# The second branch's output projection as seven half-size products instead of eight, in a hybrid decoder layer

## The chip, the cores and the metric

One core of a Trainium2 chip runs the whole layer. The time is device microseconds of one execution. An execution under the hardware profiler gives the views that are quoted here; their times are microseconds unless marked ns. The engines are PE (TensorE matmuls; PEld its weight loads), DVE (VectorE), ACT (ScalarE), POOL (GpSimd) and SP (SyncE), which here only issues transfers.

## The reference

```
h = rmsnorm(x, norm_g)
proj = h @ w_in                       # q, k, v, gates of both branches, merge logits
...
y_a = o_gla @ w_pa                    # first branch: gated linear attention
...
o_sb = stick_breaking(...)            # second branch, 8 heads of 128
o_sb = o_sb.reshape(B, T, SB_WIDTH) * jax.nn.silu(s_gate)
y_b = o_sb @ w_pb
gates = jax.nn.sigmoid(m_logits + b_gate).reshape(B, T, N_BRANCH, D_MODEL)
merged = gates[:, :, 0] * y_a + gates[:, :, 1] * y_b
x = x + merged @ w_o
return rmsnorm(x, final_g)
```

SEQ and D_MODEL are 1024, everything is float32. The change concerns `o_sb @ w_pb` and, through the buffers, `merged @ w_o`.

## The kernel before

Every float32 operand of a matmul is split into a high part (rounded to the matmul's format by ScalarE) and a low part (what is left, subtracted by VectorE), and a product takes three matmuls: high by high, high by low, low by high. Each matmul has 128 rows of contraction and 512 columns. Activations are kept transposed, with the width on the partitions, in quarters: `A11`, `A12`, `A21`, `A22` are first or second half of the tokens by even or odd blocks of 128 of the width, each a tile of 4 x 512 in high and low.

The stages follow one another on TensorE. The norm and the first values come first. Then 28 jobs of two projections each (`pair_job`, `Pairs`) run as seven half-size products with sums and differences of quarters (Strassen's scheme in Winograd's form): a job is seven units of twelve matmuls, with the sums of the weights made by GpSimd. During the first 49 units VectorE also computes the decays of the linear attention and, from unit 22 on, the sums of `w_o` that the last stage uses: `t_load` fetches two blocks of rows, `t_sum` makes four differences, `t_store` writes them to DRAM (`d_t`). The list `tjobs` says after which unit each of these is issued, in a part where the order on ScalarE and VectorE is that of the program. Then the linear attention (GLA) runs with four units between its steps, and what is left of the 196 units follows. The paired products of the linear attention's q and k multiply by a factor `f` that is loaded from `d_e` (L554).

Stick-breaking attention (L895 to L1089) goes through 64 steps, eight heads of eight blocks. A step issues the scores two steps ahead, then transposes its weights (`turn`); `values(h, 0)` multiplies the weights of the first half of the queries with v after step 4, `values(h, 1)` after step 0 of the next head. Units of two other projections, 24 matmuls each, lie between (`Line`): the gates of this branch, then `pa`, the output projection of the first branch; 26 are placed in and before this stage, and six `pa` units are left behind it, in the order of output blocks 5, 6, 7, both halves of the tokens of each.

The projection of the second branch, `pb_unit`, has 16 units: eight output blocks by two halves of the tokens, each with eight blocks of contraction and three matmuls. The gated heads come back from DRAM (`d_osb`), are split into four quarters `bq`, and each output block's weights are loaded and split two blocks ahead. `m_half` evicts a unit: it loads the second gate and the first branch's gated part (`d_gb`, `d_ma`), takes the sigmoid on ScalarE, and VectorE multiplies (L1141) and adds (L1142). After every fourth unit GpSimd makes the four sums S1, S2, S4, S3 of the merged blocks (L1152), which go to DRAM and come back for the last stage.

The output projection is seven half-size products already: items `(u, t)`, product u for block t of 128 tokens, twelve matmuls each, in an order written out by hand (`items`, `parts`, `loads`, L1343 to L1354). `parts[k]` names which high and low parts are made around item k (`o_hi` on ScalarE, L1203; `o_lo` on VectorE, L1207), `loads[k]` what is fetched. In this stage the order on ScalarE, VectorE and TensorE is that of the program; SP's order, and everything before this stage's loop, is set by the scheduler of the framework. VectorE adds a bank to the residual y (L1275); the last items scale and store the rows.

Of the kernel before, what the change touches and what calls it, by code (L numbers as in the profile page):

```python
# [15 lines left out]
P = 128  # L16
# [25 lines left out]
WARM = (13, 4)  # L42

# [56 lines left out]
def hybrid_layer(ctx: ExitStack, tc: tile.TileContext, x, norm_g, w_in, w_up, b_dec,  # L100
# [34 lines left out]
    d_t = dram_set("t", 4, [P, 4, HALF])  # L135
    d_s = {nm: dram_set("s" + nm, 2, [P, 2, HALF]) for nm in ("S1", "S2", "S3", "S4", "A22")}
# [564 lines left out]

    wt = {}
    tq_ctx = ExitStack()
    tq = tq_ctx.enter_context(tc.tile_pool(name="tq", bufs=3, reuse_waits="tile"))

    def t_load(j):
        wt[j] = tq.tile([P, 4, HALF], F32, tag="t", name="t")
        for two in range(2):
            nc.sync.dma_start(wt[j][:, 2 * two:2 * two + 2],
                              w_o[(2 * j + two) * P:(2 * j + two + 1) * P].rearrange("p (h c) -> p h c", h=2))  # L710

    def t_sum(j, i):
        dst, x1, x2_ = ((0, 1, 0), (1, 3, 1), (3, 3, 0), (2, 2, 3))[i]
        nc.vector.tensor_sub(wt[j][:, dst], wt[j][:, x1], wt[j][:, x2_])

    def t_store(j):
        nc.sync.dma_start(d_t[j][:], wt[j])

    tjobs = [[] for _ in range(49 - len(djobs))]
    for j in range(4):  # L720
        tjobs[5 * j].append((t_load, (j,)))
# [345 lines left out]
    for eb in range(KB):  # L1067
        line += ([pa(eb, 0)] if eb > 2 else []) + [pa(eb, 1)] + ([pa_load(eb + 3)] if eb + 3 < KB else [])
# [7 lines left out]
    for s, (h, i) in enumerate(steps):  # L1076
        if i % 2 == 0 and s + 4 < len(steps):
            h2, i2 = steps[s + 4]
            load_q(h2, i2 // 2)
        if i == 1 and h + 1 < SB_H:  # L1080
            load_head(h + 1)
        if s + 2 < len(steps):
            scores(*steps[s + 2])
        st.run(SB_PLAN[i][0])
        turn(h, i)
        st.run(SB_PLAN[i][1])
        if i % 4 == 0 and s:
            values(*((h, 0) if i else (h - 1, 1)))
# [5 lines left out]

    pq = ctx.enter_context(tc.tile_pool(name="pq", bufs=1, reuse_waits="tile"))
    fg = pq.tile([P, D], F32, tag="fg", name="fg", bufs=1)
    nc.sync.dma_start(fg, final_g.partition_broadcast(P))
    ssq = pq.tile([P, NT, 2], F32, tag="ssq", name="ssq", bufs=1)
    mo_ctx = ExitStack()
    mo = mo_ctx.enter_context(tc.tile_pool(name="mo", bufs=6, reuse_waits="tile"))  # L1100
    pb_ctx = ExitStack()
    pb = pb_ctx.enter_context(tc.tile_pool(name="pb", bufs=1, side="right", reuse_waits="tile"))
    bq = {k: quarter(pb, "b", f"b{k[0]}{k[1]}") for k in hq}

    def b_dma(j):
        reload_dma((d_osb[2 * j], d_osb[2 * j + 1]), j)

    def pb_load(eb):
        return load(w_pb, eb * P, ("b", eb))

    def pb_unit(eb, n):
        return unit(("b", eb), bq, n, lambda pt: m_half(pt, eb, n))

    b_dma(0)
    b_dma(1)
    st.run(1)
    reload_split(bq, 0, 0)
    b_dma(2)
    st.run(1)
    reload_split(bq, 1, 1)  # L1120
    b_dma(3)
    st.run(1)
    reload_split(bq, 2, 2)
    pb_load(0)[0]()
    st.run(1)
    reload_split(bq, 3, 3)
    pb_load(1)[0]()
    st.run()


    op = {"A11": quarter(hp, "mA11", "a11"), "A12": quarter(hp, "mA12", "a12"),
          "B11": quarter(hp, "wB11", "a22"), "B21": quarter(a21b, "wB21", "a21")}
    ms, oraw = {}, {}

    def m_half(pt, eb, n):
        j, e = divmod(eb, 2)
        o = stage().bitcast(F32)
        merge_gate(o[:, 0], d_gb, 8, eb, n)
        nc.sync.dma_start(o[:, 1], d_ma[eb][:, half(n)])
        m = ms[j, n, e] = mo.tile([P, HALF], F32, tag="m", name="m")  # L1140
        nc.vector.tensor_mul(o[:, 0], pt, o[:, 0])  # L1141
        nc.vector.tensor_add(m, o[:, 0], o[:, 1])  # L1142
        if n == 0:
            hi, lo = op[("A11", "A12")[e]]
            split(m, hi[:, j], lo[:, j])

    def m_sum(j, nm, x1, x2_, fn):

        def go():
            a, b_ = (ms[j, v] if isinstance(v, str) else ms[(j,) + v] for v in (x1, x2_))  # L1150
            ms[j, nm] = ev.tile([P, HALF], F32, tag="f", name="f")
            nc.gpsimd.tensor_tensor(ms[j, nm], a, b_, op=fn)  # L1152

        return (go, False)

    def m_sums(j):
        return [m_sum(j, "S1", (1, 0), (1, 1), ALU.add), m_sum(j, "S2", "S1", (0, 0), ALU.subtract),
                m_sum(j, "S4", (0, 1), "S2", ALU.subtract), m_sum(j, "S3", (0, 0), (1, 0), ALU.subtract)]

    def m_stores(j, nms=("S2", "S1", "S4", "S3", "A22")):  # L1160
        def go():
            for nm in nms:
                nc.sync.dma_start(d_s[nm][j // 2][:, j % 2], ms[j, nm] if nm[0] == "S" else ms[j, 1, 1])

        return (go, False)


    WQ = {"B11": (0, 0), "B21": (1, 0), "B22": (1, 1)}

    def o_load(nm, tag="raw", js=(0, 4)):  # L1170
        def go():
            raw = (raw_tile().rearrange("p k c -> p (k c)") if tag == "raw" else
                   sw.tile([P, 4, 4, P], F32, tag="tt", name="tt", bufs=1).rearrange("p q a c -> p (q a c)"))
            oraw[nm] = raw = raw.rearrange("p (j c) -> p j c", j=4)
            if nm[0] == "T":
                for j in range(4):
                    nc.sync.dma_start(raw[:, j], d_t[j][:, ("T1", "T3", "T4", "T2").index(nm)])
                return
            for i in range(2):
                n = min(js[1] - 2 * i, 2)  # L1180
                if nm in WQ:
                    e, J = WQ[nm]
                    src = (w_o.rearrange("(j two p) c -> two p j c", two=2, p=P)
                           [e][:, 2 * i:2 * i + 2, J * HALF:(J + 1) * HALF])
                else:
                    src = d_s[nm][i][:]
                nc.sync.dma_start(raw[:, 2 * i:2 * i + n], src[:, 0:n])

        return (go, False)

    def o_ends(nm, js):

        j0, n = (js, 1) if isinstance(js, int) else (js[0], 2)
        src = ms[j0, nm] if (nm, j0) in (("S2", 3), ("S1", 3)) else oraw[nm][:, j0:j0 + n]
        if n == 1:
            src = src if (nm, j0) in (("S2", 3), ("S1", 3)) else src[:, 0]
        hi, lo = (op[nm][j0 // 2] if isinstance(op[nm], list) else
                  tuple(a[:, j0:j0 + n] if n > 1 else a[:, j0] for a in op[nm]))
        return hi, lo, src
# [9 lines left out]
    def o_part(nm, i):  # L1209
        def go():  # L1210
            o_hi(nm, (2 * i, 2 * i + 1))
            o_lo(nm, (2 * i, 2 * i + 1))
# [195 lines left out]
```

## Time and profile before

| | |
|---|---|
| three runs | 1212.0, 1212.16, 1214.72 us; median 1212.16 |
| profiled execution, whole | 1212.76 us |
| its span, first to last instruction | 1211.1 us, granted clock 0.998 |
| last matmul of the first branch's six units, about | 1040 us |
| second branch's projection | about 1040 to 1127 us |
| output projection | about 1127 to 1204 us |

In lists by line, a row has line, engine, operation, output and inputs, shapes and count, then busy time in us and mean ns, then the engine's idle time before these instructions and what ended it. In lists by time, a row has start, duration, engine, line, and in brackets the idle time before. A row of waits has the waiting engine and tile, the releaser, the total in us, how often, and the longest. In the table by stage, the count of instructions stands in brackets behind each engine's busy time.

### The profile page before, as it was taken

What the parts mean: (1) busy time and instruction counts of PE and PEld (TensorE: products, weight loads), DVE (VectorE), ACT (ScalarE), POOL (GpSimd) and SP (SyncE); (2) the same over time, 40 slices, a digit from 0 to 9 for tenths busy, and PEclk for the clock granted to TensorE, in tenths of its full rate; (3) what the DMA queues carried; (4) which work ended last, traced back from release to release, by engine and by line L of the source; (5) the groups of instructions that cost most, each with busy time, mean ns of one, the idle gap of its engine ahead of it and who ended that gap; (6) DMA issues with size and microseconds to landing.
All of it is one profiled execution on the core that took longest, in us unless ns stands there. A gap on an engine that the chain in (4) does not pass through costs nothing.

```text
span 1211.1 us, 17231 instructions
## 1 busy us (share of the span) xinstructions
PE 1192.9 (99%) x6135; PEld 1005.2 (83%) x6135; DVE 791.6 (65%) x1273; ACT 538.7 (44%) x1045; POOL 316.4 (26%) x303
## 2 busy tenths in 40 slices
PE   8999999999999999999999999999999999999997
PEld 7999878888888888888888887888877888888886
DVE  6474875676766667766765428777677875345675
ACT  5344663344334444444444326454445554232343
POOL 1495523322422424323323201111121110033201
PEclk9999999999999999999999999999999999999999
DMA  7554348866646647657554295555887557667652
GB/s 280 192 149 132 148 172 293 275 212 184 203 154 203 179 134 232 218 176 239 177 170 157 74 336 168 177 169 182 285 277 237 178 178 237 191 216 255 229 202 105
DMA packets 197650, 241.37 MB, mean 199 GB/s; under 512 B 11926, under 2 KB 134828, under 8 KB 195516
## 3 DMA queue, kind: packets, MB, share of 16 engines
q1 hardware_dynamic: 196988, 239.23, 59.9%
q8 instruction: 48, 0.79, 0.3%
q10 hardware_dynamic: 576, 1.05, 0.2%
q14 instruction: 38, 0.31, 0.1%
HBM read 149.53 MB, written 90.70 MB: 198 GB/s over the span
## 4 chain that ended last, share of the span: by engine, by line
PE 91%; DVE 3%; ACT 2%; DMA 2%; issue 1%; SPq 0%; POOL 0%; ACTq 0%; DVEq 0%; POOLq 0%
PE pp L266 14%; PE pp L268 13%; PE pp L267 13%; PE pp L219 8%; PE pp L200 7%; PE pp L201 7%; PE pp L202 7%; PE av L990 1%; PE z L944 1%; PE av L991 1%; PE av L989 1%; PE tr L968 1%; PE xb L1269 1%; PE xb L1267 1%; PE xb L1268 1%
## 5 line engine op out<-in xcount | busy, mean ns | idle before, releaser
L305 DVE TENSOR_TENSOR f<-pp,f 128x512 f32<-128x512 f32 x84 | 57.8, 688 | 73.4 <-PE pp L268 72.7
L162 DVE TENSOR_TENSOR wl<-tt,wh 128x1024 fp32r<-128x1024 f32 x56 | 68.9, 1231 | 53.1 <-ACT wh L161 52.8
L953 POOL TENSOR_SCALAR_AFFINE_SELECT be<-be 128x128 f32<-128x128 f32 x64 | 37.8, 592 | 236.7 <-ACT be L949 219.1
L162 DVE TENSOR_TENSOR wl<-raw,wh 128x1024 fp32r<-128x1024 f32 x55 | 75.9, 1382 | 33.4 <-ACT wh L161 32.4
L161 ACT ACTIVATE wh<-raw 128x1024 fp32r<-128x1024 f32 x55 | 58.1, 1058 | 83.7 <-PE pp L201 37.3
L952 DVE TENSOR_TENSOR_SCAN eb<-eb,m 128x128 f32<-128x128 f32 (+3 forms) x64 | 86.5, 1353 | 9.7 <-ACT eb L948 9.7
L240 POOL TENSOR_TENSOR tt<-raw 128x512 f32<-128x512 f32 x28 | 39.1, 1398 | 200.3 <-DVE wl L162 193.7
L161 ACT ACTIVATE wh<-tt 128x1024 fp32r<-128x1024 f32 x56 | 59.3, 1059 | 67.3 <-PE pp L267 64.6
L272 ACT ACTIVATE f<-pp 128x512 f32<-128x512 f32 x84 | 49.7, 591 | 77.7 <-PE pp L268 76.3
L227 POOL TENSOR_TENSOR r<-r,nhalf 128x1 f32<-128x1 f32 x40 | 24.3, 607 | 190.2 <-DVE r L226 187.1
L948 ACT ACTIVATE eb<-z 128x384 f32<-128x384 f32 (+4 forms) x96 | 48.8, 508 | 43.3 <-issue 23.9
L587 ACT ACTIVATE o<-o,vcol 128x512 f32<-128x512 f32 x32 | 23.3, 729 | 70.8 <-DMA o<-d_gb 38.1
L956 DVE TENSOR_TENSOR be<-be,eb 128x128 f32<-128x128 f32 (+3 forms) x64 | 48.3, 755 | 3.2
L200 PE MATMUL pp<-bh,wh 128*128 128x512 f32 x128 | 49.8, 389 | 0.0
L202 PE MATMUL pp<-bh,wl 128*128 128x512 f32 x128 | 49.8, 389 | 0.0
L201 PE MATMUL pp<-bl,wh 128*128 128x512 f32 x128 | 49.8, 389 | 0.0
L949 ACT ACTIVATE be<-z 128x384 f32<-128x384 f32 (+4 forms) x96 | 49.3, 513 | 0.0
L1152 POOL TENSOR_TENSOR f<-m 128x512 f32<-128x512 f32 x8 | 14.7, 1842 | 119.1 <-DVE m L1142 119.1
L266 PE MATMUL pp<-ha11h,wh 128*128 128x512 f32 x112 | 44.6, 398 | 0.0
L266 PE MATMUL pp<-ha22h,wh 128*128 128x512 f32 x112 | 44.4, 397 | 0.2 <-DVE f L305 0.2
L266 PE MATMUL pp<-S1h,wh 128*128 128x512 f32 x112 | 44.5, 398 | 0.0
L266 PE MATMUL pp<-ha12h,wh 128*128 128x512 f32 x112 | 44.4, 396 | 0.0
(436 smaller groups left out, 3934.4 us busy)
## 6 DMA issues: line engine op xcount, KB each, us to landing
raw<-in_w_in_dram SPq DMA_DIRECT2D x31, 1024.0 KB, 6.5
d_v<-o SPq DMA_DIRECT2D x32, 256.0 KB, 3.0
d_gv<-o SPq DMA_DIRECT2D x32, 256.0 KB, 3.7
v<-d_gv SPq DMA_DIRECT2D x32, 256.0 KB, 3.1
d_ogl<-o SPq DMA_DIRECT2D x64, 128.0 KB, 2.6
d_q<-o SPq DMA_DIRECT2D x16, 512.0 KB, 4.7
d_k<-o SPq DMA_DIRECT2D x16, 512.0 KB, 4.3
k<-d_k SPq DMA_DIRECT2D x8, 1024.0 KB, 6.5
```

The lines of the kernel that those rows point to most:

```text
L161: nc.scalar.activation(hi, src, AF.Copy)
L162: eng.tensor_sub(lo, src, hi.bitcast(F32))
L200: nc.tensor.matmul(pt, whi[:, kb], h_, start=kb == 0, stop=False)
L201: nc.tensor.matmul(pt, whi[:, kb], l_, start=False, stop=False)
L202: nc.tensor.matmul(pt, wlo[:, kb], h_, start=False, stop=kb == KB - 1)
L219: nc.tensor.matmul(pt[:, 0:n], *ops[kb][i], start=k == 0, stop=k == 3 * KB - 1)
L266: nc.tensor.matmul(pt, bh[:, j], ah[:, j], start=first and j == 0, stop=False, skip_group_check=True)
L267: nc.tensor.matmul(pt, bh[:, j], al[:, j], start=False, stop=False, skip_group_check=True)
L268: nc.tensor.matmul(pt, bl[:, j], ah[:, j], start=False, stop=j == 3, skip_group_check=True)
L272: nc.scalar.activation(t[nm], t[bank], AF.Copy)
L305: nc.vector.tensor_add(add, bank, add)
L952: nc.vector.tensor_tensor_scan(rest, rest, m1[:, off:T][:, ::-1], 1.0, op0=ALU.mult, op1=ALU.max)
```

## The change

The second branch's projection becomes 28 items `(u, i)`: seven products, each over four pairs of output blocks in turn, twelve matmuls an item. Its left operands are the quarters of `o_sb` and their sums (made by GpSimd), its right ones the parts of `w_pb` with even and odd output blocks, and their sums.

The sums of `w_pb` are made beside those of `w_o`, so `t_load`, `t_sum` and `t_store` run eight times instead of four, with four buffers instead of three, one every 2.7 units, two differences per unit; and 53 instead of 49 units run ahead of the GLA part:

```
+GLA_AT = 53
...
-    d_t = dram_set("t", 4, [P, 4, HALF])
+    d_t = dram_set("t", 8, [P, 4, HALF])
...
+            if k < 4:
+                for e in range(2):
+                    nc.sync.dma_start(wt[k][:, 2 * two + e].rearrange("p (i c) -> p i c", c=P),
+                                      w_pb[rows].rearrange("p (i e c) -> p e i c", e=2, c=P)[:, e])
...
+    for k in range(8):
+        at = 27 * k // 10
+        tjobs[at].append((t_load, (k,)))
         for i in range(4):
-            tjobs[5 * j + 6 + i].append((t_sum, (j, i)))
-        tjobs[5 * j + 11].append((t_store, (j,)))
+            tjobs[at + 6 + i // 2].append((t_sum, (k, i)))
+        tjobs[at + 9].append((t_store, (k,)))
```

In stick-breaking, `values(h, 0)` moves from step 4 to step 5. The six `pa` units that are left run by half: blocks 5, 6, 7 of the first half of the tokens, then of the second.

```
-    for eb in range(KB):
-        line += ([pa(eb, 0)] if eb > 2 else []) + [pa(eb, 1)] + ([pa_load(eb + 3)] if eb + 3 < KB else [])
+    for eb in range(5):
+        line += ([pa(eb, 0)] if eb > 2 else []) + [pa(eb, 1), pa_load(eb + 3)]
+    line += [pa(eb, n) for n in range(2) for eb in range(5, KB)]
...
-        if i % 4 == 0 and s:
-            values(*((h, 0) if i else (h - 1, 1)))
+        if i == 0 and s:
+            values(h - 1, 1)
+        elif i == 5:
+            values(h, 0)
```

The operands of both projections share six places of a quarter's size (`place`, `PLACES`). Around the six `pa` units the quarters of `o_sb` and the first weights are loaded and split; the load of `final_g` stands between them, and 18 loads stand ahead of the first `pa` unit:

```
+    a_load("A11", ALL)
+    o_load("bB11")
+    a_load("A12", ALL)
+    a_load("A21", range(3))
+    a_load("A22", range(3))
+    st.run(1)
+    o_split("bA11", ALL)
+    o_split("bB11", AB)
+    o_load("bB21")
+    a_load("A21", [3])
+    a_load("A22", [3])
+    sums("b", range(3), ("S1", "S3", "S2"))
+    st.run(1)
...
```

An item's matmuls go to one of four banks `xa` or to a bank `za`. Products 0 and 2 are copied out by ScalarE (`a_keep`), product 3 too; products 1, 4, 5 and 6 end an output quarter, and VectorE merges it: add what was kept, multiply by the gate, add the first branch's part.

```
+PRODUCTS = [("A11", "B11"), ("A12", "B21"), ("S2", "T2"), ("S1", "T1"), ("S3", "T3"), ("S4", "B22"), ("A22", "T4")]
...
+    def a_merge(u, i):
+        if u not in OUT:
+            return
...
+        if u != 6:
+            t = kept["z", i] if u == 4 else kept[i]
+            nc.vector.tensor_add(t, bank, t)
+            bank = t
+        nc.vector.tensor_mul(o[:, 0], bank, o[:, 0])
+        m = oraw[nm, i] = mo_tile(where, i)
+        nc.vector.tensor_add(m, o[:, 0], o[:, 1])
+        if u == 4:
+            nc.sync.dma_start(d_s["A22"][i // 2][:, i % 2], m)
```

Both projections now have one table of parts and one of loads, numbered through: items 0 to 27 are the second branch's projection, 28 to 55 the output projection.

```
+    parts = {0: [("bS2", 0), ("bS2", 1)], 1: [("bS2", 2), ("bS2", 3)], 2: [("bT2", (0,))], 3: [("bT2", (1,))],
...
+             **{16 + j: [("bA22", j)] for j in range(4)}, **{20 + j: [("bT4", j)] for j in range(4)},
+             24: [("B11", (0,))], 25: [("B11", (1,))], 26: [("B21", (0,))], 27: [("B21", (1,))],
+             28: [("T2", (0,)), ("A12", 0)], 29: [("T2", (1,)), ("A12", 1)], 30: [("S2", 0), ("S2", 1), ("A12", 2)],
+             31: [("A12", 3)], 33: [("S2", 2), ("S2", 3)], 34: [("T1", (0,))], 35: [("T1", (1,))],
...
+    loads = {6: ("bB22", "tt"), 10: ("bT4",), 14: ("B11",), 16: ("B21", "tt"), 24: ("T2",), 26: ("T1",),
...
+    items = [(u, i) for u in range(7) for i in range(4)]
+    his(0)
+    for k, it in enumerate(items):
+        if k + 3 < len(items):
+            gate_load(*items[k + 3])
+        a_product(*it)
+        a_keep(*it)
+        a_merge(*it)
+        los(k)
+        if k + 1 < len(items):
+            gate_sig(*items[k + 1])
+        his(k + 1)
+        if k >= 24:
+            y_load(0, k - 24)
+            sums("", [k - 24], ("S1", "S3", "S2"))
```

So the sums S1, S3, S2 of the merged matrix follow the last four merges, and S4 is made during the first four items of the output projection. S1 and S2 stay in the core; S3, S4 and A22 still go through DRAM. The y tiles are loaded as whole rows, those of the second half of the tokens after item 37.

More of the change, by code (lines that the diff above doesn't have):

```diff
@@ L1102, in hybrid_layer @@
[L1102 to L1145, printed above, removed]
@@ L1191, in o_ends @@
-    def o_ends(nm, js):
[L1193 to L1199, printed above, removed]
+    mo = mo_ctx.enter_context(tc.tile_pool(name="mo", bufs=1, reuse_waits="tile"))
@@ new lines, in hybrid_layer, with part_of @@
+    st.run(1)
+    o_load("bT2", "tt")
+    nc.sync.dma_start(fg, final_g.partition_broadcast(P))
+    st.run(1)
+    o_split("bA12", ALL)
+    sums("b", [3], ("S1", "S3", "S2"))
+    o_load("bT1")
+    st.run(1)
+    o_split("bB21", AB)
+    sums("b", ALL, ("S4",))
+    o_load("bT3")
+    st.run()
+    def part_of(w, j, cols):
+        return (v[:, j % 2, cols] for v in w[j // 2]) if isinstance(w, list) else (v[:, j, cols] for v in w)
+    PRODUCTS = [("A11", "B11"), ("A12", "B21"), ("S2", "T2"), ("S1", "T1"), ("S3", "T3"), ("S4", "B22"), ("A22", "T4")]
@@ L1239, in hybrid_layer @@
     ys = {}
+    py = []
     def y_load(n, t):
[L1243 to L1251 removed]
@@ L1274, in add @@
     def add(n, t, J, bank):
-        nc.vector.tensor_add(ys[n, t][J], bank, ys[n, t][J])
+        nc.vector.tensor_add(ys[n, t][:, half(J)], bank, ys[n, t][:, half(J)])
     def square(n, t, J):
```

278 lines of the change are left out of this document (151 added, 127 removed), and 7 rows, old and new, of the table parts.

## The prediction

> **What bounds the kernel now.** I read the page first, then the stages, then single engines in order of time. The page's engine line and its costliest TensorE and GpSimd groups:
>
> ```profile
> span 1211.1 us, 17231 instructions
> PE 1192.9 (99%) x6135; PEld 1005.2 (83%) x6135; DVE 791.6 (65%) x1273; ACT 538.7 (44%) x1045; POOL 316.4 (26%) x303
> ...
> L200 PE MATMUL pp<-bh,wh 128*128 128x512 f32 x128 | 49.8, 389 | 0.0
> ```
>
> TensorE is the bound: 18.2 us of 1211.1 are not busy. Work taken from TensorE shortens the kernel only as long as nobody makes it wait. Busy time by stage (columns: stretch, its length, then each engine, granted clock, DMA share, GB/s):
>
> ```profile
> 170.00:200.00 30.00, 29.82 (x140) 24.27 (x139) 16.32 (x20) 14.36 (x20) 7.11 (x5) 1.00 0.87 307
> 600.00:850.00 250.00, 247.82 (x1244) 206.98 (x1243) 158.39 (x248) 109.73 (x242) 43.46 (x62) 1.00 0.53 176
> 1060.00:1110.00 50.00, 50.00 (x223) 41.39 (x222) 26.10 (x30) 16.14 (x20) 13.32 (x9) 1.00 0.64 218
> 1160.00:1200.00 40.00, 40.00 (x178) 33.10 (x178) 30.09 (x47) 13.41 (x28) 2.74 (x5) 1.00 0.32 119
> ```
>
> In the second branch's projection (1060 to 1110) and the output projection (1160 to 1200) TensorE has no gap at a granted clock of 1.00. The first trap is the 389 ns of a matmul: 223 of them fit in 50.00 us, so one costs about 0.22 us of the stage and its record overlaps the next. The pace is better read from the evictions in VectorE's order of time:
>
> ```profile
> 1062.34 0.69 DVE L1141 TENSOR_TENSOR o<-pp,o 128x512 f32<-128x512 f32 x1 [2.63 <-PE pp L202]
> 1063.07 0.69 DVE L1142 TENSOR_TENSOR m<-o 128x512 f32<-128x512 f32 x1
> 1063.67 1.22 DVE L162 TENSOR_TENSOR wl<-raw,wh 128x1024 fp32r<-128x1024 f32 x1
> 1067.78 0.69 DVE L1141 TENSOR_TENSOR o<-pp,o 128x512 f32<-128x512 f32 x1 [2.89 <-PE pp L202]
> ...
> 1149.38 0.69 DVE L1275 TENSOR_TENSOR y<-pp,y 128x512 f32<-128x512 f32 x1 [0.83 <-PE pp L1269]
> 1149.99 1.22 DVE L1207 TENSOR_TENSOR mS1l<-raw,mS1h 128x1024 fp32r<-128x1024 f32 x1
> ...
> 1152.10 0.69 DVE L1275 TENSOR_TENSOR y<-xb,y 128x512 f32<-128x512 f32 x1 [0.83 <-PE xb L1269]
> 1152.71 0.68 DVE L1207 TENSOR_TENSOR mS1l<-raw,mS1h 128x512 fp32r<-128x512 f32 x1
> 1153.31 0.68 DVE L1207 TENSOR_TENSOR mS1l<-f,mS1h 128x512 fp32r<-128x512 f32 x1
> 1153.91 1.22 DVE L1207 TENSOR_TENSOR wB22l<-raw,wB22h 128x1024 fp32r<-128x1024 f32 x1
> 1155.05 0.68 DVE L1275 TENSOR_TENSOR y<-xb,y 128x512 f32<-128x512 f32 x1
> ```
>
> Evictions that wait for TensorE come 5.44 us apart where a unit has 24 matmuls, 2.72 us where an item has 12: 0.227 us each. VectorE's own pace is here too, start to start: 0.61 for an add from PSUM, 0.60 for a 512-wide low part, 1.14 for a 1024-wide one, 0.73 where the next instruction needs the result.
>
> **The change part by part.** *Matmuls.* The projection had 16 units of 24 matmuls, 16 x 5.44 = 87.0 us; now 28 items of 12, 28 x 2.72 = 76.2 us. Minus 10.9 us (48 matmuls; by the 389 ns record it would be 18.7, which is wrong). All else is a question of who makes TensorE wait at 2.72 us an item. I number the items 0 to 27 (new projection) and 28 to 55 (output projection), with E(k) the end of item k's matmuls.
>
> *VectorE inside the projection.* A merge was two operations per 5.44 us; in items 16 to 23 it is now three chained ones and a 512-wide low part per 2.72: 0.73 + 0.73 + 0.61 + 0.60 = 2.67. VectorE just keeps up, so it ends with item k about when item k+1 ends. That shows once: the last low part of bT4 is issued behind the merge of item 23, and the twelfth matmul of item 24 needs it, 11 x 0.227 = 2.5 us after E(23). It is there at 0.1 + 0.73 + 0.73 + 0.61 + 0.69 = 2.9: plus 0.4 us. Items 8 to 15 ask at most 2 x 0.60 + 1.14 = 2.34 and wait for no merge: nothing.
>
> *GpSimd beside VectorE at the seam.* The sums S1, S3, S2 of the merged matrix, 12 operations, used to be spread over the projection, four per 22 us; now they follow the last four merges, three per 2.72 us, with four S4 behind them. What GpSimd and VectorE do to each other is shown where GpSimd makes such sums without a break, at 62 to 108 us, and at the one late cluster of before:
>
> ```profile
> L503 POOL TENSOR_TENSOR f<-f 128x512 f32<-128x512 f32 x12 | 19.1, 1592 | 2.7 <-DVE S3l L162 1.8
> L162 DVE TENSOR_TENSOR S4l<-f,S4h 128x512 fp32r<-128x512 f32 x3 | 4.6, 1527 | 0.2
> L162 DVE TENSOR_TENSOR S3l<-f,S3h 128x512 fp32r<-128x512 f32 x3 | 3.9, 1301 | 0.0
> L162 DVE TENSOR_TENSOR wl<-raw,wh 128x1024 fp32r<-128x1024 f32 x2 | 3.6, 1826 | 0.5 <-ACT wh L161 0.5
> L162 DVE TENSOR_TENSOR vl<-raw,vh 128x1024 fp32r<-128x1024 f32 x2 | 3.4, 1690 | 0.5 <-ACT vh L161 0.5
> L162 DVE TENSOR_TENSOR S2l<-f,S2h 128x512 fp32r<-128x512 f32 x3 | 3.1, 1039 | 0.3
> L162 DVE TENSOR_TENSOR S1l<-f,S1h 128x512 fp32r<-128x512 f32 x3 | 3.1, 1030 | 0.2
> ...
> 1086.99 1.31 POOL L1152 TENSOR_TENSOR f<-m 128x512 f32<-128x512 f32 x1 [16.45 <-DVE m L1142]
> ...
> 1131.47 2.16 POOL L1152 TENSOR_TENSOR f<-f,m 128x512 f32<-128x512 f32 x1
> ...
> 1134.64 1.28 DVE L1275 TENSOR_TENSOR y<-xb,y 128x512 f32<-128x512 f32 x2
> ```
>
> Alone a GpSimd sum takes 1.31, beside a busy VectorE 2.16. VectorE's 512-wide operations with both inputs in SBUF take 1.22 on the mean of those four groups against 0.68, its 1024-wide ones 1.76 against 1.22; adds from PSUM keep 0.64. So, start to start, I price 0.60 x 1.79 = 1.09 and 1.14 x 1.44 = 1.64 as long as GpSimd runs: 16 sums at about 2.0 are 32 us from E(24) + 1.5.
>
> VectorE's list, from E(24) as zero: item 24 multiplies from PSUM 0.73 (0.1 after the matmuls), adds 0.61, splits half of B11 1.64, done at 3.1. Items 25 to 27 cost 0.73 + 1.09 + 1.64 = 3.46 each against 2.72 of TensorE: 13.5. Items 28 and 29 (add from PSUM, half of T2, one block of A12) 0.61 + 1.64 + 1.09 = 3.34 each: 20.1. Item 30 (add, two blocks of S2, one of A12) 0.61 + 3 x 1.09 = 3.88: 24.0. Item 31 (add, last block of A12) 1.70: 25.7. TensorE ends item 31 at 7 x 2.72 = 19.0, and the twelfth matmul of item 32, the first product that uses A12, needs the last block at 19.0 + 2.5 = 21.5. It comes at 25.7: plus 4.2 us. Without any slowing the same list gives E(31) + 1.3, a cost of 0. I take 4.2, since the rows at 62 to 108 are the nearest case in which both run without a break. T2, S2 and all later parts have four or more items of lead, and the new B11 has until E(27) = 8.2 and is done at 6.6.
>
> The Trainium skill, "SBUF — State Buffer", section on the two separate sides, puts it more harshly: a VectorE instruction with two SBUF inputs and a GpSimd one that reads SBUF hold a shared port pair exclusively, and the loser blocks for the whole instruction. The adds from PSUM at 0.64 agree; 1.22 for a 512-wide one is less than a whole turn (0.68 + 1.31 = 1.99). By the rule the sum would be that of the second rival.
>
> *Transfers of the projection.* Items 16 to 27 each load two gate tiles of 256 KB; with three buffers, a load waits for the merge three items before.
>
> ```profile
> o<-d_gb SPq DMA_DIRECT2D x16, 256.0 KB, 3.5
> o<-d_ma SPq DMA_DIRECT2D x16, 256.0 KB, 4.1
> ...
> t<-in_w_o_dram SPq DMA_DIRECT2D x8, 512.0 KB, 6.4
> ...
> DMA packets 12779, 19.04 MB, mean 261 GB/s; under 512 B 687, under 2 KB 8879, under 8 KB 12392
> ```
>
> A gate may take until 3 x 2.72 + 0.85 (its multiply) - 2.2 (the freeing merge) - 1.3 (issue and sigmoid) = 5.5 us; 3.5 to 4.1 fit. From item 13 to 24 the queue carries 6 MB of gates, 2 MB of B11 and B21 and 1 MB of stores in 33 us, about 280 GB/s, beside 218 in this stage before. Cost 0, to 4 at most if landings go to 6.4.
>
> *Sums of w_pb.* Four more 1 MB loads and stores, 16 more sums on VectorE between the 23rd and the 53rd unit of paired products, while four more of these units come ahead of the GLA part instead of behind it (no work added). VectorE has the room (16.32 busy of 30.00 above). The queue is the narrow place: 179 to 252 us carried 19.04 MB at 261 GB/s (last row above); 8 MB more in some 84 us make about 340. What would be late is the factor f from d_e, behind which VectorE's evictions queue. I take 0, to 3.
>
> *Stick-breaking.* The values of the first half move behind the next step's transposes.
>
> ```profile
> PE av L990 <- DVE atl L162: 2.8, 3, 1.3
> ...
> PE z L944 <- ACT be L949: 0.9, 3, 0.3
> ```
>
> That can save the 2.8 us; but then nothing stands between the scores of steps 6 and 7, which share two banks that ScalarE empties, and 0.3 for each of eight heads would be 2.4. I take 0, from -2.8 to +2.4.
>
> *Around the first branch's last six units.* They are regrouped by half so that places come free; 18 loads (4.5 MB) now stand on SP ahead of the first one's gate. That unit's bank is needed after 3 x 5.44 = 16.3 us. Loads were issued ahead before, when buffers allowed it:
>
> ```profile
> 980.18 0.33 SPq L1251 DMA_DIRECT2D yd<-in_x_dram  x1
> ```
>
> which was two stages early, so 0, to 2. The load of final_g and the later y loads move along SP, with ten or more items of cover. The kernel's tail is untouched.
>
> Sum: -10.9 + 0.4 + 4.2 = -6.3. The profiled execution took 1212.76 (1.66 beyond its span), so 1206.5 by its time; the median of the three runs is 0.6 lower, which gives **1205.9 us**.
>
> **The rivals.** *The ports cost little:* GpSimd's sums yield, or VectorE catches up before item 32. For it: in the late cluster of before two adds from PSUM and a 512-wide part ran at full pace, and TensorE did not wait. Against it: there were four sums, here are sixteen, and VectorE has no idle time left. 1212.2 - 10.9 + 0.4 = 1201.7.
>
> *Full blocking at the seam:* VectorE and GpSimd take strict turns. Fifteen VectorE operations with SBUF inputs (three adds, twelve parts) each wait for a sum of 1.31: 19.7 us, with their own 9 x 0.60 + 6 x 1.14 = 12.2 and 1.4 before them 33.3 (the operations on PSUM run beside the sums); minus 21.5 is a stall of 11.8: 1213.5. The means of 1.22 and 1.76 speak against it. This is the rule of the Trainium skill's page named above, carried through.
>
> *Slower: the gate loads pace items 16 to 27.* When a landing L exceeds 5.5 us, each item takes (L - 5.5)/3 longer, 4 us over twelve items per us of L. With the 4.6 us of stalls above, the gain is gone from L = 5.5 + 6.3/4 = 7.1 on; at 8.5 the price is 12 and the time 1217.9. For it: 512 KB loads took 6.4 in the crowded stretch. Against: the gates themselves took 3.5 to 4.1 at 218 GB/s.
>
> That the matmuls do not go away cannot be: the counts are in the loops.
>
> **How the numbers follow.** Forecast 0.50, little port cost 0.26, full blocking 0.12, gate pace 0.12. About 0.3% (3.6 us) is what a measurement can tell from no change: faster means below 1208.5, slower above 1215.8. The forecast with its open 0 to +3, +2, +4 and -2.8 to +2.4 lies below 1208.5 in about seven of ten cases (0.35), else it is the same; the first rival gives 0.26 faster; full blocking gives 0.01 faster, 0.09 same, 0.02 slower; gate pace 0.01, 0.03 and 0.08. Together 0.63, 0.27, 0.10. The range runs from the first rival with half of stick-breaking's gain, 1200.3, to full blocking, 1213.5.
>
> **What would show it.** Right: the same 2.72 us between items; 48 matmuls fewer; TensorE waiting for the low part of A12 at item 32 for 3 to 6 us, and for bT4 at item 24 for about half a microsecond; VectorE never idle between. Wrong: no wait at the seam, a wait for a gate or a merge from item 16 on, waits in the paired products behind d_e, or new ones of z for ScalarE in stick-breaking.

## The result and the profile after

The changed kernel takes 1220.28 us (median of four runs, 1219.98 to 1222.28) against 1213.18 for the kernel before (four runs, 1212.0 to 1214.72): a ratio of 1.0059, with a 95% interval of 1.0047 to 1.0071. It is slower by 0.6%. The forecast was 1205.9, and its range ended at 1213.5.

The profiled execution took 1220.52 us at a granted clock of 0.992. The page's span and engine lines after:

```profile
span 1218.8 us, 17307 instructions
PE 1190.8 (98%) x6087; PEld 1000.3 (82%) x6087; DVE 849.3 (70%) x1323; ACT 556.1 (46%) x1079; POOL 343.0 (28%) x319
```

TensorE issues the promised 48 matmuls fewer (6135 to 6087) and is idle for 28.0 us of its span where it was idle for 18.2. The stages, marked by the first and last matmul of their source lines in the two profiled executions, say where:

| stage, us | before | after | difference | forecast |
|---|---|---|---|---|
| up to the paired products | 114.6 | 115.8 | +1.2 | 0 |
| paired products and linear attention | 602.9 | 608.6 | +5.7 | 0, to 3 |
| stick-breaking, to its last values | 290.1 | 289.9 | -0.2 | 0 |
| last six units of the first branch | 32.6 | 33.6 | +1.0 | 0, to 2 |
| second branch's projection | 87.2 | 77.2 | -10.0 | -10.5 |
| output projection | 75.5 | 86.1 | +10.6 | +4.2 |
| tail | 8.2 | 7.6 | -0.6 | 0 |

The projection gained what it should. Two stages gave it back: the output projection, and one that ends 300 us before the projection begins. (The first row is no part of it: the paired products begin between 114.5 and 116.9 us in the thirteen profiled executions of this study, with no relation to what was edited. The start goes with TensorE's granted clock between 10 and 22 us: it lies at 114.5 to 114.6 us in the six executions with 1.00 there, that of the kernel before among them, at 115.7 to 116.0 in the six with 0.86, that of the changed kernel among them, and at 116.9 in the one with 0.72.)

TensorE's waits in the changed kernel, longest total first, then one further down:

```profile
PE pp L1353 <- DVE A12l L1194: 7.5, 3, 4.0
PE pp L270 <- ACT wh L165: 2.6, 1, 2.6
...
PE xa L1247 <- DVE bT4l L1194: 0.5, 1, 0.5
```

The first and last were forecast, at 4.2 and 0.4. The middle one was taken at nothing: L270 belongs to the paired products.

**The seam.** TensorE's order of time after, from item 32's first matmul to item 34's:

```profile
1135.96 0.39 PE L1351 MATMUL pp<-B21h,A12h 128*128 128x512 f32 x1
...
1139.41 0.50 PE L1353 MATMUL pp<-B21h,A12l 128*128 128x512 f32 x1 [2.16 <-DVE A12l L1194]
...
1144.43 0.80 PE L1353 MATMUL pp<-B21h,A12l 128*128 128x512 f32 x1 [4.05 <-DVE A12l L1194]
...
1147.35 0.80 PE L1353 MATMUL pp<-B21h,A12l 128*128 128x512 f32 x1 [1.26 <-DVE A12l L1194]
1147.94 0.63 PE L1351 MATMUL pp<-B21h,A12h 128*128 128x512 f32 x1
1148.37 0.63 PE L1352 MATMUL pp<-B21l,A12h 128*128 128x512 f32 x1
...
1152.02 0.39 PE L1351 MATMUL pp<-B21h,A12h 128*128 128x512 f32 x1
```

Item 32 stops for one block of A12 after another and lasts from 1135.96 to 1147.94, 11.98 us in place of 2.72. Item 33 waits for nothing, yet it takes 4.08 us (to 1152.02): its matmuls start 0.43 us apart, not 0.227. So 9.3 us are lost in item 32 and 1.4 in item 33. The table by stage, 5 us a row and then two rows of half a microsecond (last three columns: granted clock, DMA share, GB/s), shows the clock:

```profile
1135.00:1140.00 5.00, 2.84 (x13) 2.00 (x12) 5.00 (x4) 0.00 (x0) 4.92 (x3) 1.00 0.24 88
1140.00:1145.00 5.00, 0.95 (x3) 0.50 (x2) 5.00 (x5) 0.00 (x0) 4.92 (x4) 0.55 0.06 23
1145.00:1150.00 5.00, 3.74 (x9) 2.49 (x8) 4.21 (x6) 0.88 (x3) 3.03 (x3) 0.50 0.71 272
1150.00:1155.00 5.00, 5.00 (x22) 4.06 (x21) 2.05 (x6) 2.56 (x5) 0.00 (x0) 0.92 0.84 282
```

```profile
1140.00:1140.50 0.50, 0.39 (x2) 0.00 (x0) 0.50 (x1) 0.00 (x0) 0.49 (x1) 1.00 0.00 0
1140.50:1141.00 0.50, 0.00 (x0) 0.00 (x0) 0.50 (x2) 0.00 (x0) 0.43 (x1) 0.53 0.00 0
```

The clock falls to 0.50 just after 1140.50, when the gap of 4.05 us has only begun (at 1140.38): ahead of the fall lie the gap of 2.16 us and 1.0 us of matmuls. It is back at about 1150.8 (0.73 between 1150.50 and 1151.00), some 10.2 us later.

From 1135 to 1145 VectorE is busy for all of 10 us and GpSimd for 9.84: neither is idle, both are slow. VectorE's and GpSimd's orders of time there:

```profile
1120.63 0.78 DVE L1286 TENSOR_TENSOR A<-o 128x512 f32<-128x512 f32 x1
1121.34 2.31 DVE L1194 TENSOR_TENSOR B11l<-raw,B11h 128x1024 fp32r<-128x1024 f32 x1
1123.57 0.68 DVE L1284 TENSOR_TENSOR o<-xa,o 128x512 f32<-128x512 f32 x1
1124.28 1.07 DVE L1286 TENSOR_TENSOR A<-o 128x512 f32<-128x512 f32 x1
...
1137.61 1.74 DVE L1194 TENSOR_TENSOR A12l<-A,A12h 128x512 fp32r<-128x512 f32 x1
1139.28 3.43 DVE L1194 TENSOR_TENSOR S2l<-A,S2h 128x512 fp32r<-128x512 f32 x2
1142.64 1.74 DVE L1194 TENSOR_TENSOR A12l<-A,A12h 128x512 fp32r<-128x512 f32 x1
1144.30 1.28 DVE L1359 TENSOR_TENSOR y<-xb,y 128x512 f32<-128x512 f32 x2
1145.50 1.79 DVE L1194 TENSOR_TENSOR A12l<-A,A12h 128x512 fp32r<-128x512 f32 x1
```

```profile
1118.72 2.15 POOL L1152 TENSOR_TENSOR A<-A,N 128x512 f32<-128x512 f32 x1 [64.27 <-DVE A L1286]
...
1138.88 7.86 POOL L1152 TENSOR_TENSOR A<-A,A 128x512 f32<-128x512 f32 x5
```

From start to start, a low part of 512 columns takes 1.7 us, one of 1024 columns 2.23; my list had 1.09 and 1.64. An add with both inputs in SBUF takes 1.0, where I had 1.09. Operations from PSUM keep 0.68. (Two adds to y that my list put ahead of the last block stand behind it; that was in the kernel's favour.)

**The paired products.** The stretch 200 to 280 us by stage, before and then after:

```profile
200.00:280.00 80.00, 80.00 (x366) 65.66 (x365) 55.92 (x84) 29.43 (x44) 26.93 (x25) 1.00 0.76 244
```

```profile
200.00:280.00 80.00, 76.52 (x335) 62.32 (x334) 64.84 (x88) 25.91 (x37) 25.88 (x21) 0.98 0.92 323
```

TensorE was never idle here before; now it is for 3.5 us, at a clock of 0.98, while the transfers went from 244 to 323 GB/s and their share from 0.76 to 0.92. The clock is part of the loss: in rows of 1 us it is 0.82 from 249 to 250 us, 0.50 up to 253 and 0.97 up to 254, so 0.50 for 3.4 us, which costs an estimated 1.7 us of matmuls. The chain of waits from 175 to 285 us after names the transfer that TensorE ends up behind, the factor f:

```profile
218.72 5.72 DMA f<-d_e
...
226.11 7.99 DMA f<-d_e
...
235.29 6.27 DMA f<-d_e
```

The loads of f over the whole kernel, before and then after, with the median landing last:

```profile
f<-d_e SPq DMA_DIRECT2D x16, 256.0 KB, 3.7
```

```profile
f<-d_e SPq DMA_DIRECT2D x16, 256.0 KB, 4.7
```

The longest landing of a transfer of d_e was 6.6 us before and is 8.0 after. The 80 us hide how full the queues were; two rows of 20 us, after:

```profile
200.00:220.00 20.00, 20.00 (x92) 16.55 (x91) 18.61 (x25) 6.36 (x9) 5.86 (x4) 1.00 1.02 334
220.00:240.00 20.00, 20.00 (x90) 16.57 (x89) 13.85 (x18) 5.58 (x8) 5.49 (x4) 1.00 1.02 389
```

The DMA share, 0.80 and 0.79 in these rows before, is at its end, and TensorE's gaps follow behind, from 240 us on.

### The profile page after: what moved, and what is told of

It reads as the page before. It is cut to its first block, busy times and chain, and to the rows that moved or that the text cites. A ratio compares the mean times of both kernels' runs of the same rounds, so it can differ in the third digit from the quotient of the medians.

```text
span 1218.8 us, 17307 instructions
## 1 busy us (share of the span) xinstructions
PE 1190.8 (98%) x6087; PEld 1000.3 (82%) x6087; DVE 849.3 (70%) x1323; ACT 556.1 (46%) x1079; POOL 343.0 (28%) x319
## 4 chain that ended last, share of the span: by engine, by line
PE 79%; DVE 9%; DMA 6%; ACT 3%; issue 2%; SPq 1%; POOL 0%; ACTq 0%; DVEq 0%; POOLq 0%
PE pp L270 12%; PE pp L272 12%; PE pp L271 12%; PE pp L223 8%; PE pp L204 4%; PE pp L205 4%; PE pp L206 4%; DMA f<-d_e 2%; PE av L1002 1%; PE z L955 1%; PE av L1001 1%; PE av L1000 1%; PE tr L979 1%; DMA raw<-in_w_in_dram 1%; PE z L957 1%
## 5 line engine op out<-in xcount | busy, mean ns | idle before, releaser
L964 POOL TENSOR_SCALAR_AFFINE_SELECT be<-be 128x128 f32<-128x128 f32 x64 | 40.4, 633 | 232.3 <-ACT be L960 221.1
L165 ACT ACTIVATE wh<-raw 128x1024 fp32r<-128x1024 f32 x47 | 49.7, 1060 | 80.7 <-PE pp L271 39.5
L166 DVE TENSOR_TENSOR wl<-raw,wh 128x1024 fp32r<-128x1024 f32 x47 | 67.9, 1445 | 25.0 <-ACT wh L165 20.1
L270 PE MATMUL pp<-ha11h,wh 128*128 128x512 f32 x112 | 44.8, 400 | 2.6 <-ACT wh L165 2.6
L270 PE MATMUL pp<-S3h,wh 128*128 128x512 f32 x112 | 45.0, 401 | 0.0
L270 PE MATMUL pp<-ha22h,wh 128*128 128x512 f32 x112 | 44.5, 397 | 0.2 <-DVE f L309 0.2
L270 PE MATMUL pp<-ha12h,wh 128*128 128x512 f32 x112 | 44.5, 397 | 0.0
L270 PE MATMUL pp<-S1h,wh 128*128 128x512 f32 x112 | 44.5, 397 | 0.0
L271 PE MATMUL pp<-S3l,wh 128*128 128x512 f32 x112 | 44.1, 394 | 0.0
L272 PE MATMUL pp<-S3h,wl 128*128 128x512 f32 x112 | 44.1, 394 | 0.0
L270 PE MATMUL pp<-S4h,dh 128*128 128x512 f32 x112 | 44.0, 392 | 0.0
L270 PE MATMUL pp<-S2h,wh 128*128 128x512 f32 x112 | 43.9, 392 | 0.0
```

Of the source, the lines that this page charges most:

```text
L165: nc.scalar.activation(hi, src, AF.Copy)
L166: eng.tensor_sub(lo, src, hi.bitcast(F32))
L270: nc.tensor.matmul(pt, bh[:, j], ah[:, j], start=first and j == 0, stop=False, skip_group_check=True)
L271: nc.tensor.matmul(pt, bh[:, j], al[:, j], start=False, stop=False, skip_group_check=True)
L272: nc.tensor.matmul(pt, bl[:, j], ah[:, j], start=False, stop=j == 3, skip_group_check=True)
```

## The experiments

Theory: the seam's loss is VectorE held up by GpSimd's sums in front of A12, and the paired products' loss is the 8 MB of w_pb that now move there. Rivals: VectorE's own new work (16 differences early, a longer list at the seam), the clock, the order of SP's queue. The time of a stage is that of one profiled execution. Five kernels here, the changed one among them, have the same paired products, and that stage took 608.1 to 609.8 us in them, so a difference of 1 us in it says little.

**Seam: leave out GpSimd's sums.** The 16 operations are dropped.

```
+                if pre == "":
+                    oraw[nm, j] = oraw[where or "A22", j]
+                    continue
```

> Leaves out GpSimd's sixteen sums S1, S3, S2, S4 of the merged matrix at the seam (the parts are split from the unsummed blocks); VectorE's own list stays as it is. Theory (the sums slow VectorE's low parts): the wait for A12 at item 32 is gone or under 1 us, the granted clock stays at 1.00, the output projection takes 76 to 77 us instead of 86.7, the time about 1210.5. Rival (VectorE's list is too long at 2.72 us an item even alone): a wait of 5 us or more for A12 stays, 1217 or more.

Measured 1209.45 us (1207.49 to 1210.02), ratio to the kernel before 0.9964 (0.995 to 0.9978). The stretch of the seam by stage:

```profile
1120.00:1160.00 40.00, 40.00 (x178) 33.16 (x177) 30.30 (x44) 21.04 (x33) 0.00 (x0) 1.00 0.75 266
```

TensorE has no gap, and the output projection takes 75.5 us as before. VectorE's own list, uncontended, fits, as the prediction's "without any slowing" had it. The whole 10.6 us is GpSimd beside VectorE, and what followed from it.

**Seam: make A12 first.** Same work, other order; GpSimd keeps its sums.

```
-             28: [("T2", (0,)), ("A12", 0)], 29: [("T2", (1,)), ("A12", 1)], 30: [("S2", 0), ("S2", 1), ("A12", 2)],
-             31: [("A12", 3)], 33: [("S2", 2), ("S2", 3)], ...
+             28: [("A12", 0), ("A12", 1)], 29: [("A12", 2), ("A12", 3)], 30: [("T2", (0,))], 31: [("T2", (1,))],
+             32: [("S2", 0), ("S2", 1)], 33: [("S2", 2), ("S2", 3)], ...
```

> Only the order of parts at the seam is changed: the four blocks of A12 at items 28 and 29, T2 at 30 and 31, S2 at 32 and 33. The sums and VectorE's work stay. Theory (what hurts is that A12's last block stands behind T2 and S2 while GpSimd slows each of them): the wait for A12 goes under 1 us, S2 or T2 may cost up to 2 at item 36, time 1210 to 1213. Rival (VectorE is behind as a whole, so that the order only chooses the victim): waits of 7 us in total move to T2 and S2, 1218 or more.

Measured 1209.42 us (1208.36 to 1211.37), just under the range expected, ratio 0.9969 (0.9956 to 0.9982). The same stretch by stage, the only new wait, and VectorE's four parts of A12:

```profile
1120.00:1160.00 40.00, 39.61 (x175) 32.24 (x174) 39.92 (x43) 19.67 (x32) 26.86 (x15) 1.00 0.65 215
```

```profile
PE pp L1351 <- DVE y L1359: 0.4, 1, 0.4
```

```profile
1130.18 6.88 DVE L1194 TENSOR_TENSOR A12l<-A,A12h 128x512 fp32r<-128x512 f32 x4
```

VectorE (39.92 of 40 us) and GpSimd are as busy as in the changed kernel, and the parts of A12 are as slow as there, 1.72 us each. But A12 is now ready at 1137.06, and what has been put behind it, T2 and S2, has items to spare. The output projection takes 76.3 us. Between the medians, the two rows of a table are worth 10.9 us.

**Seam: keep TensorE's clock up.** Forty matmuls whose result nobody reads are put between items 31 and 32 of the changed kernel.

```
+        if k == 4:
+            (ah, _), (bh, _) = op["A11"], op["B11"]
+            for _ in range(40):
+                nc.tensor.matmul(busy, ah[:, 0, 0:P], bh[:, 0], start=True, stop=True)
```

> The changed kernel with 40 matmuls of 128x512 more between items 31 and 32, whose results nobody reads (40 x 0.227 = 9.1 us), so that TensorE has work until VectorE has caught up. Theory (the wait costs twice, since TensorE's granted clock falls to 0.50 behind it): the clock stays at 1.00, item 33 takes 2.72 us instead of 4.08, and the kernel gets 1 to 2 us faster although it does more, 1218.3 to 1219.3. Rival (the drop of the clock costs nothing of its own, since VectorE sets the pace until item 34): 1220 to 1221.

Measured 1217.99 us (1215.9 to 1220.82), just under the range expected, ratio 1.0042 (1.0027 to 1.0057). The worst 5 us of the seam by stage:

```profile
1145.00:1150.00 5.00, 5.00 (x24) 4.14 (x23) 2.62 (x6) 1.76 (x4) 2.36 (x2) 1.00 0.87 315
```

The clock stays at 1.00, and the output projection takes 84.5 us instead of 86.1. The forty take 40 x 0.227 = 9.1 us, about as long as the wait, so they hide it and add nothing. So of the 10.6 us about 1.6 are the clock's, and the rest is the wait itself. In total time the two intervals, 1.0027 to 1.0057 here and 1.0047 to 1.0071 for the changed kernel, overlap; the stage and the clock carry this reading.

**Paired products: whose fault?** Two runs take one half each from the changed kernel: first the sixteen differences of w_pb on VectorE are left out, with all loads and stores kept,

```
+            if k >= 4:
+                tjobs[at + 6 + i // 2].append((t_sum, (k, i)))
```

> Leaves out the sixteen differences of w_pb that VectorE makes beside the paired products; all transfers stay (the stored tiles hold plain weights). Theory for the 5.7 us that the paired products and the GLA part lost (the transfers: a crowded queue and SP waiting in order make the factor from d_e late): at least half of the 2.6 us wait at 249 us stays, less than 2 us are gained, 1218.5 to 1220.5. Rival (VectorE's extra work is the cause): the waits at 249 and 277 us and the drop of the clock go, 1214 to 1215.5.

then three of the four tiles' loads and the four stores, with all differences kept.

```
+        if 0 < k < 4:
+            wt[k] = wt[0]
+            return
...
+        if k >= 4:
+            tjobs[at + 9].append((t_store, (k,)))
```

> Leaves out most transfers of the w_pb sums: one of four loads stays, no store; VectorE makes as many differences, on the one loaded tile, and the second branch's products read the sums of w_o. Theory (the transfers): the waits at 249 and 277 us and the drop of the clock go, the stage loses 0 to 1 us against before, 1214 to 1215.5. Rival (VectorE's extra work): the waits stay, 1218.5 to 1220.5.

Without the differences: 1220.29 us (1218.36 to 1221.85), ratio 1.0057, and the stage took 609.9. VectorE had less to do, and nothing was gained. Without the transfers: 1214.2 us (1213.38 to 1215.73), ratio 1.001, and the stage took 603.4 against 602.9 before. Its stretch 200 to 280:

```profile
200.00:280.00 80.00, 79.69 (x364) 65.37 (x362) 68.58 (x93) 29.39 (x44) 29.10 (x24) 1.00 0.74 247
```

VectorE does its extra work (68.58 us) and TensorE hardly stops. With the transfers, SP's waits for them go too; the runs that follow try to part the two.

**Paired products: the bytes alone.** The kernel before, without any of the change's products or sums, also loads four tiles of w_pb and stores them, with four buffers and one tile every 2.4 units, a little denser than the changed kernel's 2.7.

```
-    d_t = dram_set("t", 4, [P, 4, HALF])
+    d_t = dram_set("t", 8, [P, 4, HALF])
...
+            if j > 3:
+                for e in range(2):
+                    nc.sync.dma_start(wt[j][:, 2 * two + e].rearrange("p (i c) -> p i c", c=P),
+                                      w_pb[rows].rearrange("p (i e c) -> p e i c", e=2, c=P)[:, e])
```

> The kernel before, with all its products full size, that also loads w_pb in four more tiles and stores them, as many bytes and buffers as the changed kernel in the same 27 units, without any further sums on GpSimd or VectorE; nothing reads the stored tiles. If the transfers alone lengthen the paired products, that stage goes from 602.9 to 606-609 us and the time is 1216-1219.5, slower than before by 3 to 6 us, with a DMA share above 0.85 in the stretch 200 to 280 us. Rival: the transfers cost nothing without the sums; the time stays at 1213-1214.5.

Measured 1219.9 us (1218.59 to 1220.7), ratio 1.0055 (1.0042 to 1.0068); the stage took 610.0. Both lie just past the ranges expected. Its stretch, and VectorE's wait for f in the kernel before and then in this run:

```profile
200.00:280.00 80.00, 73.96 (x332) 59.49 (x330) 52.26 (x75) 25.31 (x38) 23.65 (x21) 1.00 0.92 320
```

```profile
DVE f L558 <- DMA f<-d_e: 3.1, 3, 2.2
```

```profile
DVE f L558 <- DMA f<-d_e: 11.9, 5, 3.9
```

The median landing of f is 3.6 us in this run against 3.7 before, so slow landings alone do not explain why f is late. The transfers alone, added to a kernel that is otherwise as it was, cost 7.1 us in this stage, as much as in the changed kernel or more.

**Paired products: fewer bytes.** The stores of w_pb's sums cut to an eighth, with A12 first; the second branch reads the sums of w_o in their place.

```
+        if k < 4:
+            nc.sync.dma_start(d_t[k][:, :, 0:64], wt[k][:, :, 0:64])
```

> A12 first, and the four stores of the w_pb sums write an eighth of their bytes (3.5 MB less; the second branch's products read the sums of w_o); every load, difference and wait on SP stays. Theory (the transfers' bytes): 3.5 of the 8 MB added gone, so 2 to 4 us gained against A12 first alone, 1205.5 to 1207.5. Rival (SP's waiting in order): 1208.5 to 1210.5.

Measured 1206.67 us (1204.67 to 1207.42), ratio 0.9942 (0.9929 to 0.9956); the stage took 604.8 us at 290 GB/s in the stretch 200 to 280. At 244, 290 and 322 GB/s there (before, this run, A12 first) the stage lost 0, 1.9 and 5.6 us; the 604.8 come from the fastest of the four executions, and between the medians the gain over A12 first is 2.75 us. VectorE's wait for f fell from 5.6 to 1.4 us. SP did not wait less for the tiles of the weight sums: 18.4 us, for differences to be stored and for stores to free a buffer, against 11.9 with A12 first. That speaks for the bytes and against SP's waiting in order.

**Paired products: keep the bytes, change their manner.** Three attempts, all with A12 first, to be compared with its 1209.42 us. ScalarE issues the stores, so that no load stands behind a waiting store in SP's order:

```
-        nc.sync.dma_start(d_t[k][:], wt[k])
+        nc.scalar.dma_start(d_t[k][:], wt[k])
```

> A12 first, and the stores of the weight sums are issued by ScalarE instead of SP: the same bytes, but SP no longer stands waiting for VectorE's differences (8.2 us in the changed kernel) with the factor loads behind. Theory that SP's waiting in order is what delays the factor: 2 us or more are gained against A12 first alone, 1205 to 1207.5. Rival (the transfers themselves, 323 GB/s at 200 to 280 us): 1208.5 to 1211.

Measured 1211.46 us (1209.37 to 1214.6), ratio 0.9985; the stage took 613.0 in the profiled execution, the slowest of ten, and VectorE's wait for f came to 11.2 us against 5.6 with A12 first. The time lies just past both ranges. By itself the run doesn't settle SP's order: SP no longer waits for the differences (9.0 us with A12 first), but for stores to free a buffer it now waits 8.7 us instead of 2.9. Why this is worse stays open.

Three buffers instead of four, which spreads the first four tiles:

```
-    tq = tq_ctx.enter_context(tc.tile_pool(name="tq", bufs=4, reuse_waits="tile"))
+    tq = tq_ctx.enter_context(tc.tile_pool(name="tq", bufs=3, reuse_waits="tile"))
```

> Changed kernel with A12 made first (1209.42) and three buffers for the sums' tiles, as the kernel before had, in place of four: the loads of the first megabytes then wait for stores, and the burst at 180-260 us, where records showed 334 to 395 GB/s, is flattened. If the burst is what makes the d_e loads late (landings of 6 to 8 us), the pairs take some 604-607 us in place of 608.6 and the time is 1205-1208. Rival: the 8 MB that are moved decide, wherever they lie in this stage; then the waits only move and the time is 1208.5-1211.

Measured 1214.21 us (1211.54 to 1217.01), ratio 1.0009 (1.0 to 1.0019). Both expectations missed: the stage took 614.0, the worst of all, with less moved in the stretch:

```profile
200.00:280.00 80.00, 73.21 (x310) 58.78 (x309) 59.69 (x81) 24.22 (x34) 24.77 (x21) 0.96 0.89 309
```

The waits for buffers delay the transfers without thinning them out much: from 180 to 260 us the DMA share was still 0.97. The fourth buffer that the change added is worth some 5 us.

Other jobs first, so that the products that need f come behind the first of these transfers:

```
-                  [gv_pair(0)] + gla_qk(0) + [gg_pair(0), gv_pair(1), gg_pair(1)] + gla_qk(1) +
+                  [gv_pair(0), gg_pair(0), gv_pair(1)] + gla_qk(0) + [gg_pair(1)] + gla_qk(1) +
```

> A12 first at the seam, and the paired products in another order: the jobs of the linear attention's first gate and second v come ahead of its first q and k, so that the jobs which load the factor from d_e run at units 42 to 55, mostly behind the loads and stores of the weight sums. Theory (late factors are the link by which the crowded queue stops VectorE and so TensorE): the paired products and the GLA part lose 0 to 2 us against before instead of 5.7, 1204.5 to 1207.5. Rival (any job in the crowded stretch is stopped, by its weights or its stores): 1208.5 to 1210.5 as with A12 first alone.

Measured 1208.41 us (1206.93 to 1209.85), ratio 0.9959 (0.9946 to 0.9971): the stage went to 606.1, but stick-breaking, which comes next, to 292.6. There TensorE waited once, 2.1 us, for a load of q from d_q, and the granted clock was 0.79 from 878 to 886 us. Most of the expected gain did not come: the time is outside the theory's range and just under the rival's.

**The first branch's units.** TensorE waits 0.8 us for the first one's gated values in the changed kernel, 1.0 with A12 first. Six of the 18 loads (the expectation says eight) are moved behind that unit, with A12 first:

```
+    st.run(1)
     a_load("A21", range(3))
     a_load("A22", range(3))
...
-    st.run(1)
```

> Changed kernel with A12 made first, and the eight loads of A21 and A22 of the first branch issued behind the first unit of its projection instead of ahead of it. If the wait of that unit for its gated values (1.0 us in the run with A12 first, 0.8 us in the changed kernel) is due to the loads ahead of the gate's own, it goes, and the time is 1208-1209 against 1209.4. Rival: the gate's loads are late for another reason; the wait stays and the time is 1209-1210.

Measured 1210.07 us (1208.27 to 1211.31), ratio 0.9973 (0.9962 to 0.9984). The wait is gone in this run, but of the other kernels that have the 18 loads ahead, six show no such wait either, and three do. The time lies just past both ranges. What decides the wait stays open; it is worth 1 us.

## Why the prediction was wrong

**Right.** The matmuls: -10.0 us in the stage against -10.9 + 0.4 forecast; the pace of 0.227 us, not the 389 ns of a record, was the right reading. The wait for bT4 came at item 24, 0.5 us long; with the wait the item lasted 3.45 us instead of 2.72, 0.7 in place of my 0.4. The gates never made TensorE wait, as forecast, and with them the rival that had them pace items 16 to 27 falls. Stick-breaking stayed where it was, at -0.2. The loss around the first branch's units (+1.0) lies within its bound.

**Wrong, the step that failed most: the price of the seam.** The place, the tile and the mechanism were right; the size was 10.6 instead of 4.2 us. The step was "I take 4.2, since the rows at 62 to 108 are the nearest case in which both run without a break". They don't. VectorE by stage there, in the kernel before:

```profile
62.00:108.00 46.00, 46.00 (x386) 46.00 (x385) 28.88 (x34) 16.27 (x32) 41.49 (x26) 1.00 0.55 161
```

GpSimd is busy for 41.49 of 46 us, but VectorE for only 28.88. The means of 1.22 and 1.76 us mix instructions that came alone and instructions that followed one another. Where VectorE had several in a row, 1.98 and 1.77 us against 2.31 and 1.74 at the seam, its order of time in the kernel before in places already came near the seam's price:

```profile
84.70 0.41 DVE L162 TENSOR_TENSOR o<-pp,o 128x256 fp32r<-128x256 f32 x1
85.04 1.98 DVE L162 TENSOR_TENSOR vl<-raw,vh 128x1024 fp32r<-128x1024 f32 x1
86.94 1.77 DVE L162 TENSOR_TENSOR S4l<-f,S4h 128x512 fp32r<-128x512 f32 x1
```

Not everywhere: two 1024-wide parts in a row took 3.58 us together at 81.21. So that the idle share explains the gap between the two prices is argued from these rows; no run varies it. With the durations of the seam itself the list is done 30.4 us after E(24) (1116.89 to 1147.29), where I had 25.7 and the rival of full blocking 33.3. Needed at 21.5, the last block is 8.9 us late. (A slip in the list, 0.60 x 1.79 = 1.09 where it is 1.07, moves it by 0.1 us.)

The Trainium skill, "SBUF — State Buffer", section on the two separate sides, has the loser wait for the whole instruction of the other. A strict turn would give 0.68 + 1.31 = 1.99 and 1.22 + 1.31 = 2.53; the trace shows 1.74 and 2.31. The rule was nearer than the means that I preferred to it, and too harsh by a seventh at 512 columns and a tenth at 1024.

**Missing: the clock.** I had no term for what a long wait does to what comes after it. At the seam it is 1.6 us, and in the paired products of the profiled execution an estimated 1.7. The Trainium skill, "TensorE: Matmul & The Clock Gate", Part 1, says that about 3.4 us of idleness halve the clock and as much activity restores it; the trace agrees on the second in the paired products (0.50 for 3.4 us while matmuls ran on), and not on the first. There one gap of 2.6 us was enough; at the seam the clock fell 0.15 us into the gap of 4.05, with no gap longer than 2.16 ahead of it; and in the run with the bytes alone a gap of 3.2 us left it at 1.00. At the seam it was back 6.3 us after the matmuls went on at 1144.43, with another gap of 1.26 us in between.

**Wrong by half: the sums of w_pb.** "I take 0, to 3" became +5.7. I had the rate about right (323 GB/s measured, 340 worked out, though its own figures, 261 and 8 MB in 84 us, make 356) and named what would be late, f behind d_e. I gave it no price, because VectorE had room; but VectorE's room is no cover when what it waits for is a transfer, and a mean of 340 over 84 us left out that the DMA share stands at 1.02 from 200 to 240 us. The runs show the cause, since the loss goes with the transfers (603.4), stays without the differences (609.9) and comes with the transfers alone (610.0). That it is f that TensorE meets first is read from the chain. The run with small stores speaks against a fault of SP's order, and no run singles out f: VectorE waited for it 6.0 us with three buffers, where the stage took 614.0, and 7.2 with the jobs reordered, where it took 606.1. How the crowded transfers reach TensorE stays open in part.

Together: 5.7 and 10.6 - 4.2 = 6.4 are 12.1 of the 14.4 us between 1205.9 and 1220.28. Of the rest, 1.2 is where the paired products begin and 1.0 the first branch. None of my rivals had the sign: the one on the slow side was about the gates, whose loads kept their time. The run with A12 first and small stores, 1206.67, is close to the forecast; it has the change's matmuls and neither of the two losses in full.

**What the change is worth.** With its two rows in another order it takes 1209.42 us, 0.3% less than the kernel before (0.9956 to 0.9982), and with the jobs reordered 1208.41 (0.9946 to 0.9971). The two intervals overlap widely. The 5.7 us that are left in the paired products are the price of moving the sums of w_pb through DRAM in the stage where transfers were densest.

## What to carry to other kernels

Price a contended operation by rows in which both engines have a queue, not by the mean of a group: check the busy share of both in the window that the mean comes from. When an engine becomes the narrow place for a few items, order its list by due time first; that added no work here and gave back more than the whole gain of the change. And look at what a change moves elsewhere, in the stage where the DMA share is already high: the loads that wait there may belong to a product that the change never touches.

## What was not expected of the hardware

Beside an unbroken run of GpSimd sums, a VectorE subtraction of two SBUF inputs takes 1.74 us at 512 columns (0.68 alone) and 2.31 at 1024 (1.22 alone), while GpSimd's sums take 1.6 to 2.3 (1.31 alone); operations from PSUM keep 0.68. The length of a gap alone does not decide TensorE's clock: it fell to 0.50 with a gap of 2.1 us in the run with reordered jobs and with one of 2.6 us in the changed kernel, and stayed at 1.00 with gaps of 2.7 and 3.2 us in the runs without the seam's sums and with the bytes alone. It was 0.50 for 3.4 us in the paired products and for 10.2 us at the seam. Loads of 256 KB on the chain of waits took 5.7 to 8.0 us where the core moved 334 to 389 GB/s at a DMA share of 1.02; the median of the sixteen is 4.7 us, 3.7 in the kernel before.
